# Pool starts moved by 128 bytes, and raw buffers taken from a ring, in a two-layer encoder kernel

## The chip, the cores and the metric

The kernel runs on one core of one Trainium2 chip. The metric is device time in microseconds: the median of several executions, and for the traces one execution that the hardware profiler recorded. A core has five engines with an instruction queue each: TensorE (PE; its weight loads are listed apart as PEld), VectorE (DVE), ScalarE (ACT), GpSimd (POOL) and SyncE (SP, which here issues nearly all DMAs).

## The reference

Two layers over 256 tokens of width 2048, in fp32. Each layer has a token mixer and a gated feed-forward, both between RMS norms, with a residual:

```python
x = x + rms_norm_post(mixer(rms_norm_pre(x)))
x = x + rms_norm_post(conv_glu(rms_norm_pre(x)))

def conv_glu(h, w_up, conv_w, conv_b, w_down):      # width 5632
    u = h @ w_up
    gate, val = u[..., :D_FF], u[..., D_FF:]
    gate = depthwise_conv3(gate, conv_w, conv_b)
    return (gelu(gate) * val) @ w_down
```

Layer 0's mixer is dilated and grouped-query attention with one input and one output projection. Layer 1's is latent attention: `c = h @ w_in` gives a latent query (512 columns), a latent key-value (512) and a rotary key (64), which are normed and projected up; then come attention and the output projection.

## The kernel before

**Products.** An fp32 matrix is parted into a high and a low half (`hi`, `lo`), and each product is made of three matmuls: high by high, low by high, high by low (`mm3`, lines 219 to 221; in `down`, lines 1312, 1313 and 1315). In the token-major products (`proj_tok`, the output projections and `down`) the activations are the stationary operand, 128 columns at a time, and the weights stream past, 512 columns each: a row `ps<-whi,gh` has `whi` streaming and `gh` stationary. The stationary tiles are `xhl` (normed input of a sub-layer), `oh`/`ol` (heads of a mixer), `cq`/`ckv` (the latents), `gh`/`gl` (the feed-forward's gated values, nine tiles each, and `g_last` for the last two blocks) and `seven` (sums of token blocks, below). In `proj_t` (lines 236 and 238) the weights are stationary.

**Down.** The down product uses Strassen's scheme of seven products for 11 of its 22 pairs of row blocks in the first half of the columns (h = 0) and 13 in the second (h = 1). `block_sums` makes the sums of weight blocks beforehand and writes them to DRAM (`b`); `token_sums` makes the sums of token blocks on VectorE into `seven` tiles. Their homes are the `x` tiles and `xm` tiles of the pool `act` and the tile `st` of the feed-forward's own pool. `down_order` sets the order of the plain and the seven-product items; `units` are the indices of the seven-product items.

**Weights.** All weights come in chunks of 128 x 1024 in one list. `weights()` hands out the next chunk; ahead of it, `_split` parts three chunks: ScalarE casts `raw` to `whi` (line 159), VectorE subtracts to get `wlo` (line 154). `_load` issues the DMA of later chunks on SP (line 137) into one of four `raw` buffers, or one of the extra tiles listed in `self.more` (then called `raw_more`): in `down` the tiles `yf`, `gw`, `misc` of the feed-forward's pool, in the second half of `down` also `x1` to `x3` once their sums are used up (line 1320), and at mixer 1's start four tiles of its own pool (`oh2`, `ol2`, `oh3`, `ol3`). Which one is taken is a running count modulo the number of buffers (line 130).

**Pools.** `const`, `act`, `wp` and `small` are opened first and stay; each mixer and each feed-forward opens a pool after them (`mix0`, `ffn0`, `mix1`, `ffn1`), which starts where `small` ends. Tiles in `small` take a multiple of 32 bytes per partition, for each of their buffers. `pre_norm` takes four small columns there, one of them `floor` with four buffers (line 366). The stationary tiles in the late pools start 128 bytes past a multiple of 256 (`gh0` at 117632), those in `act` at a multiple.

**Order.** The tile framework sorts the instructions of each engine; a tile of a late pool can be written only when what lay there before was used for the last time. At mixer 1's start the first eight matmul groups read weights that were parted ahead into tiles of the feed-forward's pool (`ahead`), and the transposes of the new `x` (line 482) run between them.

Of the kernel before, what the change touches and what calls it, by code (L numbers as in the profile page):

```python
# [3 lines left out]

# [1 line left out]

# [54 lines left out]
class Model:  # L61
# [6 lines left out]
    def __init__(self, ctx, tc, a, out):  # L68
        self.tc, self.nc, self.a, self.out = tc, tc.nc, a, out
        self.soon, self.bg, self.running = [], deque(), []  # L70
        self.held = deque()
        self.gate, self.lead, self.led = (), None, 8
        pool = lambda name, **k: ctx.enter_context(tc.tile_pool(name=name, **k))
        self.const = pool("const", bufs=1)
        self.act = pool("act", bufs=1)
        self.wp = pool("wp", bufs=1)
        self.small = pool("small", bufs=2)
        self.ps = pool("ps", bufs=4, space=bass.MemoryType.PSUM)
        self.dram = pool("dram", bufs=1, space=bass.MemoryType.DRAM)
        self.blocks = {}  # L80
        self.more, self.turns = [], count()


    def now(self, gen, after=()):
# [41 lines left out]
    def _load(self, i):  # L126
        if i >= len(self.chunks) or i in self.loaded or i < self.at or i in self.made:
            return
        src = self.chunks[i]() if callable(self.chunks[i]) else self.chunks[i]
        turn = next(self.turns) % (4 + len(self.more))  # L130
        if turn < len(self.more):
            pool, tag = self.more[turn]
            raw = pool.tile([P, 1024], F32, tag=tag, name="raw_more", bufs=1)
        else:
            raw = self.wp.tile([P, 1024], F32, tag="raw", name="raw", bufs=4)
        raw = raw[:, :src.shape[-1]]
        self.nc.sync.dma_start(out=raw, in_=src)
        self.loaded[i] = raw
# [25 lines left out]
            return low  # L164

    def less(self):
        self.more = []

    def behind(self, instructions):

# [5 lines left out]
    def weights(self, upto=None):  # L176

        i = self.at
        if upto is None:
            upto = i + (2 if self.lead else 3)  # L180
            self.follow()
        for j in range(i, upto):
            self._split(j)
        for j in range(upto, i + 6 + len(self.more)):
            self._load(j) if j < upto + 4 + len(self.more) else None
        self.at += 1
        return self.made.pop(i)

# [161 lines left out]
    def pre_norm(self, sp=None):  # L350

        nc = self.nc
        yield
        ss = self.small.tile([P, 2, 4], F32, tag="ss", name="ss", bufs=2)
        for c in range(4):
            while self.led <= 2 * c:
                yield
            for t in range(2):
                with self.behind(self.gate):
                    self.square_sums(ss[:, t, c:c + 1], self.x[c][:, t, :])  # L360
            yield
        tot, v, s = self.col("tot", 2), self.col("prev", 2), self.col("pres", 2)
        self.r = self.col("prer", 2)
        nc.vector.tensor_reduce(out=tot, in_=ss, op=ALU.add, axis=AX.X)
        nc.vector.tensor_scalar(out=v, in0=tot, scalar1=1.0 / D, scalar2=EPS, op0=ALU.mult, op1=ALU.add)
        self.floor = self.col("floor", 2, 4)
        nc.vector.tensor_scalar(out=self.floor, in0=v, scalar1=EPS, scalar2=None, op0=ALU.mult)
        nc.scalar.activation(s, v, AF.Sqrt)
        self.heron(s, v, self.r)
# [556 lines left out]
    def mixer1(self, pre):  # L926
        nc, tc, a = self.nc, self.tc, self.a
        with tc.tile_pool(name="mix1", bufs=1) as sp:
            x, xs = self.x_parts(), self.xhl
# [9 lines left out]
            def latent(ps, row, out):  # L939
                g = sp.tile([P, 512], F32, tag="grow", name="grow", bufs=1)  # L940
                nc.sync.dma_start(out=g, in_=a["lat"][row:row + 1, :].broadcast_to([P, 512]))
                ss = self.small.tile([P, 2, 1], F32, tag="ls", name="ls", bufs=2)
                for t in range(2):
                    self.square_sums(ss[:, t, :], ps[t])
                rr = self.rstd_over(ss, self.r, 1, 512)
                whole = []
                for t in range(2):
                    y = sp.tile([P, 512], F32, tag="y", name="y", bufs=2)
                    nc.vector.scalar_tensor_tensor(out=y, in0=ps[t], scalar=rr[:, t, :], in1=g,
                                                   op0=ALU.mult, op1=ALU.mult)  # L950
                    whole.append(y)
                yield
                for k in range(0, 4, 2):
                    pt = self.psum("at").rearrange("p (i t) -> p i t", i=2)
                    for j in range(2):
                        for t in range(2):
                            self.turn_whole(pt[:, j, t * P:(t + 1) * P], whole[t][:, (k + j) * P:(k + j + 1) * P])
                    self.parted(out[:, k:k + 2, 0, :], out[:, k:k + 2, 1, :], pt)
# [81 lines left out]
                        yield  # L1040

            norm = self.now(self.pre_norm())
            self.more = [(sp, f"{n}{i}") for i in range(2, 4) for n in ("oh", "ol")]
            evq = self.evac(latent(self.proj_tok(KD, x, opening=True), 0, cq), 2, (norm,))
            evkv = self.evac(latent(self.proj_tok(KD, x, before={6: self.less}), 1, ckv), 2, (evq,))
            evkr = self.evac(evac_kr(proj_kr()), 1, (evkv,))
# [2 lines left out]
            for p in range(8):  # L1049
# [3 lines left out]
                if p % 2 == 0:  # L1053
                    v, v_gen = [], []
# [140 lines left out]
    def token_sums(self, seven, homes, gh, gl, upto, room, room_tag, bufs=1, pause=10):  # L1195

        def add(out, a, b, op=ALU.add):
            self.nc.vector.tensor_tensor(out=out, in0=a, in1=b, op=op)

        while len(seven) < upto:  # L1200
            p = len(seven)
            pool, tag, q = homes.pop(0)
            k = slice(2 * (p % 2), 2 * (p % 2) + 2 * q)
            tmp = room.tile([P, 2, 512 * q], F32, tag=room_tag, name="sums", bufs=bufs)
            add(tmp[:, 0], gh[p // 2][:, k].rearrange("p k t -> p (k t)").bitcast(F32),
                gl[p // 2][:, k].rearrange("p k t -> p (k t)").bitcast(F32))
            a = tmp[:, 0].rearrange("p (q k t f) -> p q k t f", q=q, k=2, t=2)
            s = tmp[:, 1].rearrange("p (q n f) -> p q n f", q=q, n=4)
            a11, a12, a21, a22 = (a[:, :, k, t] for t in range(2) for k in range(2))
            add(s[:, :, 0], a21, a22)  # L1210
            add(s[:, :, 1], s[:, :, 0], a11, ALU.subtract)
            add(s[:, :, 2], a11, a21, ALU.subtract)
            add(s[:, :, 3], a12, s[:, :, 1], ALU.subtract)
            yield
            home = pool.tile([P, q, 4, 2, P], F32R, tag=tag, name=f"seven{p}")
            self.parted(home[:, :, :, 0, :], home[:, :, :, 1, :], s)
            seven.extend(home[:, i] for i in range(q))
            for _ in range(pause):
                yield

    def down(self, gh, gl, post, pre, kept, seven, sums):
# [5 lines left out]
        m, gains = [], []  # L1227
        many = PAIRS[0 if pre else 1]

        self.more = [(self.room, t) for t in ("yf", "gw", "misc")]  # L1230

        def x_back():
            for c in range(4):
                self.x[c] = self.act.tile([P, 2, 512], F32, name=f"x{c}")
                nc.sync.dma_start(out=self.x[c], in_=kept[c])
# [52 lines left out]
        for h in range(2):  # L1288
            items = down_order(h, many[h])
            units = [n for n, item in enumerate(items) if item[0] == "seven"]  # L1290
# [4 lines left out]
            n = len(items) - held  # L1295
# [20 lines left out]
                return ins if group else None  # L1316

            for i in range(n):
                if h and i == units[20]:
                    self.more += [(self.act, f"x{c}") for c in (1, 2, 3)]  # L1320
                    self.now(sums(many[1], self.wp, "raw", 4))
                if h and i == units[-1] - 6:
                    self.more = []
                if h and i == units[-1]:
                    x_back()
                if i == units[0]:
                    banks += [self.psum("at") for _ in range(4)]
                w = self.weights()
                while items[i][0] == "seven" and len(seven) <= items[i][1]:
                    self.tick()  # L1330
                for t in range(2):
                    products(i, t, w)
                self.tick()
                if i == units[-1]:
                    m.append(self.act.tile([P, 2, 2, 512], F32, tag="xm2" if h else "xm3", name=f"m{h}"))
                    if h:
                        gains.append(self.gain_row(post, 3))
                    ended = self.now(done(h, 0, added(h, banks[4:])))
# [152 lines left out]
```

## Time and profile before

| | us |
|---|---|
| median of 3 runs | 2051.09 (2050.76 to 2052.47) |
| profiled execution | 2049.91 |
| its span, first to last instruction | 2047.8 |

The page of the profile gives, for each engine, busy time, its share of the span and the count of instructions; then the chain of work that ended last; then the costliest groups of instructions by line, engine, operation and tiles (`out<-in`), with busy time, the mean of one, and the idle time ahead of them with what ended it. Timeline rows read: start, duration, engine, line, operation, tiles, count, and in brackets the idle time before with what was waited for. "DMA to landing" rows of a view by tile give the time from a DMA's issue to its last byte, least, median and most. Durations of matmuls are modelled and overlap; the distance of two starts is recorded.

### The profile page before, as it was taken

How to read it: one execution, taken by the hardware profiler on the slowest of the kernel's cores; microseconds unless marked ns; L12 is line 12 of the kernel's file. 1: busy time of each engine (PE TensorE's matmuls, PEld its weight loads, DVE VectorE, ACT ScalarE, POOL GpSimd, SP SyncE). 2: the span in 40 equal slices, each digit the busy share in tenths (PEclk: the TensorE clock that was granted, in tenths of full speed). 3: DMA queues.
4: the chain of work that ended last, by engine and by line, in shares of the span. 5: the costliest groups of instructions: out<-in, count | busy, mean ns of one | idle time of the engine just before them, and what ended most of it. 6: DMA issues, size and time to landing. Idle time of an engine off the chain costs nothing.

```text
span 2047.8 us, 29869 instructions
## 1 busy us (share of the span) xinstructions
PE 2035.3 (99%) x10858; PEld 1737.3 (85%) x10858; DVE 1577.6 (77%) x2368; ACT 1177.0 (57%) x1837; POOL 0.2 (0%) x4
## 2 busy tenths in 40 slices
PE   9999999999999999999999999999999999999998
PEld 7888888888888888888778998888888888888886
DVE  6877757887777787868787875688877777797876
ACT  7654546655555555656665664565555555555664
POOL 0000000000000000000000000000000000000000
PEclk9999999999999999999999999999999999999999
DMA  9545566888888887888964445688888988878895
GB/s 335 181 149 162 164 195 232 297 277 327 296 300 307 287 316 268 272 291 300 350 215 167 137 129 168 200 303 290 307 291 294 317 290 310 298 253 278 293 370 192
DMA packets 152499, 532.83 MB, mean 260 GB/s; under 512 B 16928, under 2 KB 17440, under 8 KB 152352
## 3 DMA queue, kind: packets, MB, share of 16 engines
q1 hardware_dynamic: 152064, 530.65, 75.9%
q8 instruction: 85, 1.39, 0.3%
q14 instruction: 62, 0.51, 0.1%
q10 hardware_dynamic: 288, 0.28, 0.0%
HBM read 474.23 MB, written 56.62 MB: 259 GB/s over the span
## 4 chain that ended last, share of the span: by engine, by line
PE 98%; ACT 1%; DVE 0%; DMA 0%; issue 0%; DVEq 0%; SPq 0%
PE ps L236 31%; PE ps L238 15%; PE ps L221 8%; PE ps L219 8%; PE ps L220 8%; PE ps L1312 7%; PE ps L1313 7%; PE ps L1315 7%; PE ps L652 1%; PE ps L305 1%; PE ps L555 1%; PE ps L482 0%; PE ps L562 0%; DMA raw<-in_w_in 0%; ACT whi L159 0%; PE ps L988 0%
## 5 line engine op out<-in xcount | busy, mean ns | idle before, releaser
L154 DVE TENSOR_TENSOR wlo<-raw,whi 128x1024 fp32r<-128x1024 f32 (+1 forms) x667 | 793.4, 1198 | 343.0 <-ACT whi L159 338.5
L159 ACT CAST whi<-raw 128x1024 fp32r<-128x1024 f32 (+1 forms) x667 | 684.8, 1031 | 590.9 <-PE ps L236 296.6
L236 PE MATMUL ps<-xhl,whi 128*128 128x512 f32 x2752 | 952.6, 394 | 0.0
L238 PE MATMUL ps<-xhl,wlo 128*128 128x256 f32 x2752 | 757.5, 277 | 0.0
L236 PEld LDWEIGHTS ps<-xhl,whi 128*128 128x128 f32 x2752 | 513.9, 188 | 117.1
L238 PEld LDWEIGHTS ps<-xhl,wlo 128*128 128x128 f32 x2752 | 516.5, 188 | 2.6
L154 DVE TENSOR_TENSOR wlo<-raw_more,whi 128x1024 fp32r<-128x1024 f32 (+1 forms) x129 | 144.9, 1144 | 49.4 <-ACT whi L159 48.2
L159 ACT CAST whi<-raw_more 128x1024 fp32r<-128x1024 f32 (+1 forms) x129 | 124.8, 985 | 77.4 <-PE ps L1313 48.0
L1312 PE MATMUL ps<-whi,gh 128*128 128x512 f32 x400 | 158.2, 396 | 1.1 <-ACT whi L159 1.1
L1313 PE MATMUL ps<-whi,gl 128*128 128x512 f32 x400 | 158.2, 395 | 0.0
L219 PE MATMUL ps<-whi,xhl 128*128 128x512 f32 x336 | 132.3, 395 | 0.5 <-ACT whi L159 0.5
L220 PE MATMUL ps<-wlo,xhl 128*128 128x512 f32 x336 | 131.3, 391 | 0.0
L221 PE MATMUL ps<-whi,xhl 128*128 128x512 f32 x336 | 131.0, 391 | 0.1
L1315 PE MATMUL ps<-wlo,gh 128*128 128x512 f32 x400 | 129.1, 394 | 0.0
L1168 DVE TENSOR_TENSOR blocks<-blocks 128x1024 f32<-128x1024 f32 x144 | 124.5, 865 | 0.9
L219 PE MATMUL ps<-whi,oh 128*128 128x512 f32 x256 | 101.6, 397 | 0.0
L221 PE MATMUL ps<-whi,ol 128*128 128x512 f32 x256 | 101.0, 395 | 0.0
L220 PE MATMUL ps<-wlo,oh 128*128 128x512 f32 x256 | 101.0, 394 | 0.0
L1312 PEld LDWEIGHTS ps<-whi,gh 128*128 128x128 f32 x400 | 75.3, 188 | 19.3 <-ACT whi L159 2.2
L1313 PEld LDWEIGHTS ps<-whi,gl 128*128 128x128 f32 x400 | 75.4, 189 | 17.7
L1315 PEld LDWEIGHTS ps<-wlo,gh 128*128 128x128 f32 x400 | 75.2, 188 | 17.9 <-DVE wlo L154 0.3
L309 ACT COPY gw<-ps 128x256 f32<-128x256 f32 x176 | 64.3, 369 | 39.6 <-PE ps L236 31.2
(232 smaller groups left out, 2368.1 us busy)
## 6 DMA issues: line engine op xcount, KB each, us to landing
raw<-in_w_up SPq DMA_DIRECT2D x352, 512.0 KB, 5.1
blocks<-in_w_down SPq DMA_DIRECT2D x96, 512.0 KB, 6.1
b<-blocks SPq DMA_DIRECT2D x96, 512.0 KB, 5.3
raw<-in_w_in SPq DMA_DIRECT2D x84, 512.0 KB, 4.4
raw<-in_w_down SPq DMA_DIRECT2D x71, 512.0 KB, 5.6
raw<-in_w_out SPq DMA_DIRECT2D x64, 512.0 KB, 4.0
raw_more<-in_w_down SPq DMA_DIRECT2D x57, 512.0 KB, 5.5
raw<-b SPq DMA_DIRECT2D x51, 512.0 KB, 5.9
```

Source lines behind the costliest of these rows:

```text
L154: return nc.vector.tensor_tensor(out=lo[:, s], in0=raw[:, s], in1=hi[:, s].bitcast(F32), op=ALU.subtract)
L159: self.nc.scalar.copy(hi[:, s], raw[:, s])
L219: mm(ps, lh, rh, start=start, stop=False)
L220: mm(ps, lh, rl, start=False, stop=False)
L221: return mm(ps, ll, rh, start=False, stop=stop)
L236: ins = mm(out[i], hi[:, s[kk]], x(k), start=k == 0, stop=False, skip_group_check=opening)
L238: ins = mm(out[i][:, :T], lo[:, s[kk]], x(k)[:, :T], start=False, stop=k == nk - 1, skip_group_check=opening)
L309: self.nc.scalar.copy(b, ps[:, T:])
L1168: nc.vector.tensor_tensor(out=x[:, a:a + n], in0=x[:, b:b + n] if n > 512 else x[:, a:a + n], in1=x[:, a:a + n] if n > 512 else x[:, b:b + ...
L1312: mm(bank, xh, w[0][:, c], start=start, stop=False, skip_group_check=loose)
L1313: mm(bank, xl, w[0][:, c], start=False, stop=False, skip_group_check=loose)
L1315: ins = mm(bank, xh, w[1][:, c], start=False, stop=stop, skip_group_check=loose)
```

## The change

Three edits. First, `floor` is no column of its own any more: `prev` has four columns, of which the last two are the floor; 4 buffers of 32 bytes go from `small`, and every pool opened after it starts 128 bytes lower (`gh0` at 117504, a multiple of 256). Second, the count modulo the number of buffers gives way to a deque: `ring[0]` is taken and the ring turned by one; extra tiles are put in front of it (`extendleft`, so in reversed order), and `less()` makes a ring of the four raw buffers again. Third, in the second half of `down` the late token sums start at unit 13 (unit 20 before), with their temporary in `x1` and not in a raw buffer; they are finished at unit 17, where `x1` to `x3` join the ring. The count of instructions on PE, ACT and DVE stays.

```diff
-        self.more, self.turns = [], count()
+        self.ring = deque([None] * 4)
@@ _load
-        turn = next(self.turns) % (4 + len(self.more))
-        if turn < len(self.more):
-            pool, tag = self.more[turn]
+        if self.ring[0]:
+            pool, tag = self.ring[0]
             raw = pool.tile([P, 1024], F32, tag=tag, name="raw_more", bufs=1)
         else:
             raw = self.wp.tile([P, 1024], F32, tag="raw", name="raw", bufs=4)
+        self.ring.rotate(-1)
@@ less
-        self.more = []
+        self.ring = deque([None] * 4)
@@ weights
-        for j in range(upto, i + 6 + len(self.more)):
-            self._load(j) if j < upto + 4 + len(self.more) else None
+        for j in range(upto, min(i + 2, upto) + len(self.ring)):
+            self._load(j)
@@ pre_norm
-        tot, v, s = self.col("tot", 2), self.col("prev", 2), self.col("pres", 2)
+        tot, both, s = self.col("tot", 2), self.col("prev", 4), self.col("pres", 2)
+        v, self.floor = both[:, :2], both[:, 2:]
@@
-        self.floor = self.col("floor", 2, 4)
         nc.vector.tensor_scalar(out=self.floor, in0=v, scalar1=EPS, scalar2=None, op0=ALU.mult)
@@ mixer1
-            self.more = [(sp, f"{n}{i}") for i in range(2, 4) for n in ("oh", "ol")]
+            self.ring.extendleft((sp, f"{n}{i}") for i in range(2, 4) for n in ("oh", "ol"))
@@ token_sums
-            for _ in range(pause):
+            for _ in range(pause if len(seven) < upto else 0):
                 yield
@@ down
-        self.more = [(self.room, t) for t in ("yf", "gw", "misc")]
+        self.ring.extendleft((self.room, t) for t in ("yf", "gw", "misc"))
@@
-                if h and i == units[20]:
-                    self.more += [(self.act, f"x{c}") for c in (1, 2, 3)]
-                    self.now(sums(many[1], self.wp, "raw", 4))
+                if h and i == units[13]:
+                    late = self.now(sums(many[1], self.act, "x1"))
+                if h and i == units[17]:
+                    self.finish(late)
+                    self.ring.extendleft((self.act, f"x{c}") for c in (1, 2, 3))
                 if h and i == units[-1] - 6:
-                    self.more = []
+                    self.less()
```

The order moves at a few places. The rows give line, operation, tiles with their numbers, shape and what is waited for; lines of the changed kernel are one lower. SP's queue at mixer 1's start, before. `raw_10016` to `raw_10022` are chunks 4 to 7 of layer 1's input, `raw_more_10024` to `raw_more_10030` chunks 8 to 11:

```order
L137 DMA raw_10016<-in_w_in1 128x1024 [waits DMAHW2_49,DVE_49]
L137 DMA raw_10018<-in_w_in1 128x1024 [waits DMAHW7_49,DMAHW3_49,DVE_49]
L137 DMA raw_10020<-in_w_in1 128x1024 [waits DMAHW4_49,DVE_49]
L435 DMA gb_11904<-in_post 128x512
L137 DMA raw_10022<-in_w_in1 128x1024 [waits DMAHW5_49,DVE_49]
L435 DMA gb_11906<-in_post 128x512 [waits DVE_49]
L137 DMA raw_10171<-in_w_in1 128x1024 [waits DMAHW6_49,DVE_49]
L934 DMA tabC_10009<-in_ropeC 128x256 [waits PE_49]
L137 DMA raw_more_10024<-in_w_in1 128x1024
L137 DMA raw_more_10026<-in_w_in1 128x1024 [waits DMAHW7_49]
```

And after, where `raw_more_10014` to `raw_more_10020` are chunks 4 to 7:

```order
L136 DMA raw_10022<-in_w_in1 128x1024 [waits DMAHW2_49,DVE_49]
L136 DMA raw_10024<-in_w_in1 128x1024 [waits DMAHW7_49,DMAHW3_49,DVE_49]
L136 DMA raw_10026<-in_w_in1 128x1024 [waits DMAHW4_49,DVE_49]
L434 DMA gb_11901<-in_post 128x512
L136 DMA raw_10028<-in_w_in1 128x1024 [waits DMAHW5_49,DVE_49]
L434 DMA gb_11903<-in_post 128x512 [waits DVE_49]
L933 DMA tabC_10007<-in_ropeC 128x256 [waits PE_49]
L136 DMA raw_more_10014<-in_w_in1 128x1024
L136 DMA raw_more_10016<-in_w_in1 128x1024 [waits DMAHW6_49]
```

Chunks 4 to 7 moved behind `tabC`, the first DMA into mixer 1's pool, whose wait is one for PE; chunks 8 to 11 moved ahead of it.

SP's queue in the second half of layer 0's down, where `x1` to `x3` have just become extra buffers, before (`b01` are sums of weight blocks; tile numbers rise in the order in which the chunks are used):

```order
L137 DMA raw_9327<-in_w_down0 128x512 [waits DMAHW4_49,DVE_49]
L137 DMA raw_more_9333<-b01_7_7008 128x1024 [waits DMAHW3_49]
L137 DMA raw_more_9351<-b01_7_7008 128x1024 [waits PE_49]
L137 DMA raw_more_9372<-in_w_down0 128x512 [waits DMAHW5_49,PE_49]
L137 DMA raw_more_9384<-in_w_down0 128x1024 [waits DMAHW6_49,PE_49]
L137 DMA raw_more_9329<-in_w_down0 128x1024 [waits DMAHW7_49,DMAHW0_49,DVE_49]
L137 DMA raw_9396<-b01_8_7195 128x1024
```

And after:

```order
L136 DMA raw_9289<-in_w_down0 128x512 [waits DMAHW6_49,DVE_49]
L136 DMA raw_more_9301<-in_w_down0 128x1024 [waits PE_49]
L136 DMA raw_more_9303<-b01_6_6810 128x1024 [waits DMAHW7_49]
L136 DMA raw_more_9305<-b01_6_6810 128x1024 [waits DMAHW0_49]
L136 DMA raw_more_9307<-in_w_down0 128x512 [waits DMAHW1_49,DVE_49]
```

Before, `raw_more_9329` stood behind four loads that are used after it; after, the loads stand in the order of their use, and the extra tiles come three units earlier.

VectorE's queue at the start of layer 0's down, before (`sums` are token sums; `raw_8042` is chunk 5 of the down):

```order
L701 TENSOR_TENSOR g_last_8008<-misc_3141,g_last_8008 128x256 [waits Activation_49] x2
L154 TENSOR_TENSOR wlo_8108<-raw_8042,whi_8107 128x1024 [waits DMAHW1_49,PE_49]
L154 TENSOR_TENSOR wlo_8130<-raw_8044,whi_8129 128x1024 [waits DMAHW2_49,PE_49,Activation_49]
L1198 TENSOR_TENSOR sums_8240<-gh3_3125,gl3_3134 128x1024
L1198 TENSOR_TENSOR sums_8240<-sums_8240 128x2x128 [waits DVE_49]
L154 TENSOR_TENSOR wlo_8142<-raw_more_8046,whi_8141 128x1024 [waits DMAHW5_49,PE_49,Activation_49]
```

And after, where chunk 5 lies in `raw_more_8040`, the tile `misc`:

```order
L700 TENSOR_TENSOR g_last_8006<-misc_3140,g_last_8006 128x256 [waits Activation_49] x2
L1197 TENSOR_TENSOR sums_8238<-gh3_3124,gl3_3133 128x1024
L1197 TENSOR_TENSOR sums_8238<-sums_8238 128x2x128 [waits DVE_49]
L1197 TENSOR_TENSOR sums_8238<-sums_8238 128x2x128
L1197 TENSOR_TENSOR sums_8238<-sums_8238 128x2x128 [waits DVE_49] x2
L700 TENSOR_TENSOR seven6_8256<-sums_8238,seven6_8256 128x8x128 [waits Activation_49]
L1197 TENSOR_TENSOR sums_8391<-gh4_3125,gl4_3134 128x1024 [waits DVE_49]
L153 TENSOR_TENSOR wlo_8106<-raw_more_8040,whi_8105 128x1024 [waits DMAHW6_49,PE_49,Activation_49]
```

Chunk 5's subtraction moved behind the sums; its buffer is now the one that `g_last` is made from.

More of the change, by code (lines that the diff above doesn't have):

```diff
@@ L2 @@
 from contextlib import ExitStack
-from itertools import count
 import numpy as np
```

## The prediction

> **What bounds the kernel now.** I read the page first: busy shares, clock, and the chain of waits.
>
> ```profile
> span 2047.8 us, 29869 instructions
> PE 2035.3 (99%) x10858; PEld 1737.3 (85%) x10858; DVE 1577.6 (77%) x2368; ACT 1177.0 (57%) x1837; POOL 0.2 (0%) x4
> PEclk9999999999999999999999999999999999999999
> PE 98%; ACT 1%; DVE 0%; DMA 0%; issue 0%; DVEq 0%; SPq 0%
> ```
>
> TensorE is busy for 99% of the span at a full clock and makes up 98% of the chain that ended last. So a term of my sum is worth something only if it shortens the distance from one matmul's start to the next, or opens or closes a gap on TensorE. The page's busy time of one matmul (some 390 ns) is modelled and overlaps the next, so I take the **pitch**: first and last start of an unbroken run in the timeline of PE, divided by the steps between them. The table of windows gives the counts.
>
> ```profile
> 181.60 0.39 PE L219 MATMUL ps<-whi,xhl 128*128 128x512 f32 x1
> 197.71 0.39 PE L221 MATMUL ps<-whi,xhl 128*128 128x512 f32 x1
> 256.81 0.39 PE L219 MATMUL ps<-whi,oh 128*128 128x512 f32 x1
> 326.30 0.39 PE L221 MATMUL ps<-whi,ol 128*128 128x512 f32 x1
> 181.60:197.70 16.10, 16.10 (x73) 13.33 (x72) 11.42 (x16) 5.73 (x7) 0.00 (x0) 1.00 0.55 176
> 256.80:326.30 69.50, 69.50 (x301) 56.35 (x300) 38.13 (x43) 32.87 (x44) 0.00 (x0) 1.00 0.67 207
> ```
>
> (Columns of the last two rows: window, its length, busy time and count of PE, PEld, DVE, ACT, POOL, then clock, DMA share, GB/s.) Same three lines of code, same shape, no gap in either: 72 matmuls with xhl stationary start over 16.11 us, that is 16.11 / 71 = 226.9 ns each; 300 with oh and ol over 69.49 us, 69.49 / 299 = 232.4 ns. The stationary operand is the second name. In the program xhl starts at a multiple of 256 bytes in its partition, oh and ol 128 bytes past one. In the down product the same pair exists side by side: two tiles of one shape, used by the same lines, the first (seven8) at a multiple of 256, the second (seven10, in tile st of the feed-forward's pool) 128 past one.
>
> ```profile
> 913.78 0.39 PE L1315 MATMUL ps<-wlo,seven 128*128 128x512 f32 x1
> 915.82 0.40 PE L1315 MATMUL ps<-wlo,seven 128*128 128x512 f32 x1
> 929.02 0.39 PE L1315 MATMUL ps<-wlo,seven 128*128 128x512 f32 x1
> 931.11 0.39 PE L1315 MATMUL ps<-wlo,seven 128*128 128x512 f32 x1
> ```
>
> Nine steps each: 2.04 / 9 = 226.7 ns and 2.09 / 9 = 232.2 ns. Hence **5.4 ns a matmul** hang on something that these two classes differ in. The confound: in the kernel before, every stationary operand that lies 128 past a multiple also lies above 117 KB in the partition, and every one at a multiple lies below 54 KB. The trace cannot part alignment from height; for alignment speaks that the slow pitch is flat over that height (232.4 with oh and ol, 232.2 with seven10).
>
> **Term 1, the shift.** Merging the column floor into prev takes 4 buffers of 32 bytes out of the small pool, so every pool opened after it (mixers and feed-forwards) starts 128 bytes lower: gh0 goes from 117632 to 117504 = 459 x 256, and with it gl, st, g_last, oh, ol, cq, ckv and the 256-column operands. What uses them 512 wide, from the groups by line:
>
> ```profile
> L1312 PE MATMUL ps<-whi,gh 128*128 128x512 f32 x400 | 158.2, 396 | 1.1 <-ACT whi L159 1.1
> L219 PE MATMUL ps<-whi,oh 128*128 128x512 f32 x256 | 101.6, 397 | 0.0
> L1312 PE MATMUL ps<-whi,g_last 128*128 128x512 f32 x64 | 25.4, 398 | 0.0
> L219 PE MATMUL ps<-whi,ckv 128*128 128x512 f32 x32 | 12.7, 398 | 0.0
> L219 PE MATMUL ps<-whi,cq 128*128 128x512 f32 x16 | 6.5, 405 | 0.0
> ```
>
> Each has two sister lines with the same count (each product of the program is made of three): 3 x (400 + 256 + 64 + 32 + 16) = 2304. The 72 with seven10 and some 64 steps that lead from an aligned operand into one of these bring 2440. At the difference of the long runs that is 2440 x 5.4 = 13.2 us. The shorter pair allows less within its rounding: (0.05 - 0.01) / 9 = 4.4 ns, 10.7 us. Short runs with waits between them are what the down consists of, so I take the middle, **-12.0 us** (-13.2 to -10.7). The 2752 matmuls of L236 keep their addresses. No other engine's durations hang on this: a subtraction takes 1.22 us from a raw tile of either class.
>
> A rule speaks against this term. The Trainium skill, "TensorE: Matmul & The Clock Gate", section "Step-by-step: what each phase is for", gives TensorE two independent SBUF read ports, one for the streamed operand, one for weight loads, so that loading the next tile takes nothing from the running matmul. By it the place of a stationary operand changes no pitch and term 1 is zero (rival A). The rows above disagree: 5.4 ns at equal loads and shapes.
>
> **Term 2, a late load that goes.** The old turn counter is taken modulo a length; when three tiles join in the second half of layer 0's down, the order jumps, and one load is issued five issues late (the order rows of the change show raw_more_9329).
>
> ```profile
> 983.03 0.33 SPq L137 DMA_DIRECT2D raw_more<-in_w_down  x1
> 987.67 2.00 ACT L159 CAST whi<-raw_more 128x1024 fp32r<-128x1024 f32 x2 [5.29 <-PE ps L1315]
> 987.25 0.39 PE L1315 MATMUL ps<-wlo,seven 128*128 128x512 f32 x1
> 988.77 0.50 PE L1312 MATMUL ps<-whi,gh 128*128 128x512 f32 x1 [1.14 <-ACT whi L159]
> ```
>
> ScalarE sat idle for 5.29 us, last for this load, and TensorE's step here is 1.52 us against 0.23: 1.29, with 0.1 behind it **-1.4 us**. The ring loads in turn, and no other cast in that half keeps TensorE waiting, so I see nothing late next. The sums that move from unit 20 to 13 are the same instructions, and the three tiles they join with were read for the last time two units earlier: nothing, or at worst the 0.3 us of a wait (kept in the range).
>
> **Term 3, a new wait at mixer 1's opening.** In the kernel before, weight chunks 4 to 7 of layer 1's input go into the four raw tiles and are there by 1062.82, where the cast starts. In the changed one the ring gives them the four tiles of mixer 1's own pool; these loads stand on SP behind tabC, the first DMA into that pool, which waits for TensorE's last use of the feed-forward's tiles.
>
> ```profile
> 1065.14 0.33 SPq L137 DMA_DIRECT2D raw<-in_w_in  x1
> 1065.59 0.36 SPq L934 DMA_DIRECT2D tabC<-in_ropeC  x1
> 1065.99 1.92 SPq L137 DMA_DIRECT2D raw_more<-in_w_in  x4
> DMA to landing us min/median/max: 3.7/3.7/3.7
> DMA to landing us min/median/max: 5.3/5.3/5.3
> 1062.82 1.99 ACT L159 CAST whi<-raw 128x1024 fp32r<-128x1024 f32 x2
> 1065.75 0.48 PE L219 MATMUL ps<-whi,xhl 128*128 128x512 f32 x1
> 1069.97 0.39 PE L219 MATMUL ps<-whi,xhl 128*128 128x512 f32 x1
> ```
>
> (The landing rows are those of the raw load at 1065.14 and of the first raw_more load at 1065.99.) Today chunk 4 starts on TensorE at 1065.75 and chunk 5 at 1069.97. After, chunk 4's load is issued at 1065.99 at the earliest, with nothing queued ahead, and lands 3.7 to 5.3 us later (as the raw load did; as the raw_more one did, which had that load ahead of it): 1069.7 to 1071.3. Cast 1.05, low part 1.22: its third matmul, the first with the low part, can start at 1072.0 to 1073.6, and the ten from there on at 0.23 bring chunk 5 to 1074.3 to 1075.9. That is 4.3 to 5.9 us late, all of it on TensorE. I take **+4.8**, nearer the unloaded row. Queued behind on ScalarE is nothing that TensorE needs sooner. Later the same stage gives something back:
>
> ```profile
> 1085.41 1.41 DVE L949 SCALAR_TENSOR_TENSOR y<-ps,rr,grow 128x512 f32<-128x512 f32 x2 [0.99 <-DMA grow<-in_lat]
> 1086.26 0.30 PE L305 MATMUL ps<-ident,y 128*128 128x128 f32 x1 [0.92 <-issue]
> ```
>
> This 0.9 us waits for grow, which will be there; but y's transposes now come 5 matmuls sooner after the products, so I book **-0.3** (-0.9 to +0.3).
>
> **Term 4, the two down starts.** Extra tiles now come first in the ring, the last-freed one (misc) first of all. In layer 0 chunk 5's load therefore waits for the last read of misc, and on DVE the sums move ahead of its subtraction.
>
> ```profile
> 822.11 0.39 PE L1312 MATMUL ps<-whi,gh 128*128 128x512 f32 x1
> 828.08 0.75 DVE L701 TENSOR_TENSOR g_last<-misc,g_last 128x256 fp32r<-128x256 f32 x2
> 834.66 0.39 PE L1312 MATMUL ps<-whi,gh 128*128 128x512 f32 x1
> 1822.58 1.05 ACT L159 CAST whi<-raw_more 128x1024 fp32r<-128x1024 f32 x1 [1.86 <-DMA raw_more<-in_w_down]
> 1823.68 0.50 PE L1312 MATMUL ps<-whi,gh 128*128 128x512 f32 x1
> DMA to landing us min/median/max: 5.6/5.6/5.6
> ```
>
> The read ends at 828.83; with 3.7 us to land (the free queue above) or 5.6 (the load of this chunk in layer 1, the last row) and a cast of 1.05, whi is there at 833.6 to 835.5. TensorE wants it 12.5 us after the down's start, at 834.66, and 0.25 us sooner by term 1; its low part, 1.22 us behind whi, it wants four matmuls later. So 0 to 1.5 us; I take **+1.0**, near the slow end, since layer 1 has this order already, and there the cast at 1822.58 waited for the load, and TensorE for the cast (the row at 1823.68 is stretched to 0.50). In layer 1 that stall grows by what TensorE gains ahead of it, 54 steps of 5 ns: **+0.25**.
>
> **The sum.** -12.0 - 1.4 + 4.8 - 0.3 + 1.0 + 0.25 = **-7.65 us** on the profiled execution (2049.91 us, its span 2047.8). That run lies 1.2 us under the median of 2051.09; the median then comes to **2043.4 us**. The best ends (-13.2 - 1.4 + 4.3 - 0.9 + 0 + 0.2) give -11.0, the worst (-10.7 - 1.1 + 5.9 + 0.3 + 1.5 + 0.4) -3.7: 2040.1 to 2047.4.
>
> **Rivals.** A: *the place does nothing.* The 5.4 ns belong to height, or to which operand the products take, and the pools end 128 bytes lower without result; this is also the case that the change does not do what it says. What is left is term 3, whose price then decides: -1.4 + 4.8 - 0.3 + 1.25 = +4.35, **2055.4, slower**. It turns from "no change" to "slower" where chunk 4's load lands after about 1069.9. For it speaks the confound and the rule cited; against it seven8 beside seven10.
> B: *the opening's loads are covered.* If tabC's release comes earlier than today's 1065.59, by as much as chunk 4 needs, term 3 vanishes: **2038.6**. Against it: the release is TensorE's own matmul, four transposes ahead of chunk 4.
> C: *VectorE takes over in the downs.*
>
> ```profile
> 822.10:837.70 15.60, 15.60 (x70) 12.65 (x69) 15.57 (x26) 9.72 (x16) 0.00 (x0) 1.00 0.78 255
> ```
>
> In a down's first 15.6 us DVE is busy 15.57. Were it so throughout, the gain on the downs' 1530 or so matmuls (7.5 us) would turn into waits: 2050.9; for half of them, **2047.2**. Over the whole span DVE has 77%, so only stretches can go this way.
>
> **How the numbers follow.** Forecast 0.68, A 0.17, B 0.07, C 0.08. 0.2% is 4.1 us, about what a measurement here can tell from no change: faster is under 2047.0, slower above 2055.2. The forecast's interval lies below 2047.0 but for its last tenths, so faster gets 0.66 + 0.07 + 0.02 = 0.75; A splits at its bound, slower 0.10; the rest, 0.15, is same. The range takes in the forecast, B and C, 0.83 in all: 2038.6 to 2051.
>
> **What would show it.** Right: unbroken runs with oh, ol, gh, gl at 227 ns and L236's pairs unchanged; no idle row at TensorE near 987; a gap of 4 to 6 us on TensorE ahead of chunk 4 of layer 1's input, ended by a cast whose load was issued behind tabC; a cast waiting for raw_more at layer 0's down start. Wrong: pitch still 232 (then A), no gap at the opening (B), or new waits of TensorE for wlo in the downs (C).

## The result

| | us | ratio to before, 95% interval |
|---|---|---|
| before, 5 runs | 2052.47 (2050.76 to 2055.09) | |
| changed, 5 runs | 2042.50 (2040.74 to 2043.64) | 0.9951 [0.9937, 0.9966] |
| forecast | 2043.4 (2038.6 to 2051.0) | |

The changed kernel is 0.5% faster. Its profiled execution took 2041.99 us, against 2049.91 before. Two further executions of the kernel before (2053.15 and 2055.09 us) are in its median here, which stood at 2051.09 when the forecast of -7.65 us was made; timed again beside one another (run 10), the two kernels are 7.7 us apart.

Page of the changed kernel:

```profile
span 2039.7 us, 29854 instructions
PE 2021.8 (99%) x10858; PEld 1737.4 (85%) x10858; DVE 1577.7 (77%) x2368; ACT 1177.8 (58%) x1837; POOL 0.2 (0%) x4
PE 95%; DVE 2%; DMA 2%; ACT 1%; issue 0%; SPq 0%; DVEq 0%; ACTq 0%
```

TensorE is still busy all along and DVE did nothing more; but 5% of the chain of waits now belongs to DMA, DVE and ACT, against 1% before. The span fell by 8.1 us, and the n-th matmul of one trace can be set against the n-th of the other, since both have 10858 (36 of them in another order). The lead is how much earlier the n-th matmul starts in the changed kernel; the texts below call this comparison "matched starts". Where the lead grows (-) and shrinks (+):

| stretch (time before, us) | lead, us |
|---|---|
| up to layer 0's down start (825) | -2.05 |
| its first chunks (825 to 840) | +0.54 |
| up to 983 | -3.07 |
| the place of the late load (983 to 990) | -1.50 |
| up to the end of that down | -1.19 |
| crossing into layer 1 (1045 to 1049) | +0.91 |
| mixer 1's opening (1061 to 1094) | +4.84, with -0.11 ahead of it |
| mixer 1, its projection and feed-forward | -1.90 |
| into layer 1's down (1781 to 1831) | -0.20 |
| the rest of it | -4.36 |

The gains lie where stationary tiles of the late pools are used, and at the place of the late load; the losses lie at three places. Runs with oh and ol, and the nine steps with seven10, in the timeline of PE of the changed kernel:

```profile
256.43 0.40 PE L218 MATMUL ps<-whi,oh 128*128 128x512 f32 x1
324.23 0.40 PE L220 MATMUL ps<-whi,ol 128*128 128x512 f32 x1
925.51 0.39 PE L1314 MATMUL ps<-wlo,seven 128*128 128x512 f32 x1
927.55 0.39 PE L1314 MATMUL ps<-wlo,seven 128*128 128x512 f32 x1
```

67.80 / 299 = 226.8 ns and 2.04 / 9 = 226.7 ns, where it was 232.4 and 232.2. The losses, as PE's and ACT's timelines show them (two rows of layer 0's down start, one of layer 1's, three of the crossing, the rest of the opening; SP's issue of tabC and DVE's x are among them):

```profile
831.91 2.95 ACT L158 CAST whi<-raw_more 128x1024 fp32r<-128x1024 f32 x3 [1.79 <-DMA raw_more<-in_w_down]
833.01 0.50 PE L1311 MATMUL ps<-whi,gh 128*128 128x512 f32 x1 [0.51 <-ACT whi L158]
1820.10 0.50 PE L1311 MATMUL ps<-whi,gh 128*128 128x512 f32 x1 [0.18 <-ACT whi L158]
1038.29 1.05 ACT L158 CAST ahead<-raw 128x1024 fp32r<-128x1024 f32 x1 [1.80 <-DMA raw<-in_w_in]
1041.53 1.42 DVE L473 SCALAR_TENSOR_TENSOR x<-m,postr,x 128x512 f32<-128x512 f32 x2
1042.34 0.66 PE L481 MATMUL ps<-ident,x 128*128 128x128 f32 x4 [0.85 <-DVE x L473]
1059.13 0.33 SPq L933 DMA_DIRECT2D tabC<-in_ropeC  x1
1063.39 1.04 ACT L158 CAST whi<-raw_more 128x1024 fp32r<-128x1024 f32 x1 [0.42 <-DMA raw_more<-in_w_in]
1064.49 0.73 PE L218 MATMUL ps<-whi,xhl 128*128 128x512 f32 x2 [4.51 <-ACT whi L158]
1065.75 0.79 PE L219 MATMUL ps<-wlo,xhl 128*128 128x512 f32 x1 [0.53 <-DVE wlo L153]
1066.77 0.63 PE L218 MATMUL ps<-whi,xhl 128*128 128x512 f32 x1
1067.19 0.63 PE L219 MATMUL ps<-wlo,xhl 128*128 128x512 f32 x1
1068.84 0.39 PE L218 MATMUL ps<-whi,xhl 128*128 128x512 f32 x1
1069.52 0.39 PE L218 MATMUL ps<-whi,xhl 128*128 128x512 f32 x1
```

tabC is issued at 1059.13, 6.46 us sooner than before (1065.59), so that much was TensorE's lead; chunk 5 starts at 1069.52 against 1069.97, a lead of 0.45. So 6.0 us are lost here. There are two parts: 4.51 and 0.53 us of waiting for chunk 4, whose load came behind tabC, and then a slow clock: from 1065.75 to 1068.84 seven steps take 3.09 us, where seven at 0.227 take 1.59, and the step from 1066.77 to 1067.19 is 0.42. The table of windows shows what share of the full clock was granted (third number from the end: 0.83, then 0.54, and 0.50 over the stretch of 3.41 us in which it was low):

```profile
1064.00:1066.00 2.00, 0.99 (x3) 0.55 (x4) 1.53 (x2) 2.00 (x5) 0.00 (x0) 0.83 0.93 377
1066.00:1069.00 3.00, 3.00 (x8) 2.38 (x9) 2.63 (x6) 2.99 (x7) 0.00 (x0) 0.54 0.95 288
1065.30:1068.71 3.41, 2.96 (x7) 2.38 (x8) 3.04 (x7) 3.40 (x8) 0.00 (x0) 0.50 0.94 321
```

The Trainium skill, "TensorE: Matmul & The Clock Gate", section "HAM oscillation — how this bites in real kernels", says that idle gaps of over some 3.4 us put TensorE back to half its clock. This gap of 4.5 us agrees. It isn't a bound from below, though: in run 5 half the clock followed a gap of 2.35 us.

### The profile page after: what moved, and what is told of

Read it like the earlier page. It is cut to its first block, busy times and chain, and to the rows that moved or that the text cites. A ratio compares the mean times of both kernels' runs of the same rounds, so it can differ in the third digit from the quotient of the medians.

```text
span 2039.7 us, 29854 instructions
## 1 busy us (share of the span) xinstructions
PE 2021.8 (99%) x10858; PEld 1737.4 (85%) x10858; DVE 1577.7 (77%) x2368; ACT 1177.8 (58%) x1837; POOL 0.2 (0%) x4
## 4 chain that ended last, share of the span: by engine, by line
PE 95%; DVE 2%; DMA 2%; ACT 1%; issue 0%; SPq 0%; DVEq 0%; ACTq 0%
PE ps L235 30%; PE ps L237 15%; PE ps L219 9%; PE ps L220 8%; PE ps L218 8%; PE ps L1311 7%; PE ps L1312 7%; PE ps L1314 7%; PE ps L651 2%; PE ps L304 1%; PE ps L554 1%; DVE wlo L153 1%; DMA raw_more<-in_w_down 1%; DMA raw<-in_w_in 0%; PE ps L481 0%; PE ps L561 0%
## 5 line engine op out<-in xcount | busy, mean ns | idle before, releaser
L153 DVE TENSOR_TENSOR wlo<-raw,whi 128x1024 fp32r<-128x1024 f32 (+1 forms) x659 | 783.5, 1197 | 341.3 <-ACT whi L158 334.9
L158 ACT CAST whi<-raw 128x1024 fp32r<-128x1024 f32 (+1 forms) x659 | 676.4, 1032 | 575.7 <-PE ps L235 301.0
L235 PE MATMUL ps<-xhl,whi 128*128 128x512 f32 x2752 | 952.6, 394 | 0.0
L237 PE MATMUL ps<-xhl,wlo 128*128 128x256 f32 x2752 | 757.5, 277 | 0.0
L235 PEld LDWEIGHTS ps<-xhl,whi 128*128 128x128 f32 x2752 | 513.9, 188 | 116.9
L237 PEld LDWEIGHTS ps<-xhl,wlo 128*128 128x128 f32 x2752 | 516.7, 188 | 2.6
L153 DVE TENSOR_TENSOR wlo<-raw_more,whi 128x1024 fp32r<-128x1024 f32 (+1 forms) x137 | 154.0, 1144 | 42.9 <-ACT whi L158 38.2
L158 ACT CAST whi<-raw_more 128x1024 fp32r<-128x1024 f32 (+1 forms) x137 | 134.0, 990 | 78.8 <-PE ps L1312 58.3
```

The source lines that it names most:

```text
L153: return nc.vector.tensor_tensor(out=lo[:, s], in0=raw[:, s], in1=hi[:, s].bitcast(F32), op=ALU.subtract)
L158: self.nc.scalar.copy(hi[:, s], raw[:, s])
L235: ins = mm(out[i], hi[:, s[kk]], x(k), start=k == 0, stop=False, skip_group_check=opening)
L237: ins = mm(out[i][:, :T], lo[:, s[kk]], x(k)[:, :T], start=False, stop=k == nk - 1, skip_group_check=opening)
```

## The experiments

Two questions were open. Does the shift bring the gain, and why (alignment of the stationary tile, its height, something else)? And what do the ring and the moved sums cost or save, each alone? Runs 1 to 4, 5 to 8 and 9 to 11 were timed in three sessions, each with the kernel before beside them (medians of 2050.83, 2050.78 and 2050.53 us). Each ratio is against that median; a difference to the changed kernel is one to its 2042.50 us, which run 10 found at 2042.83.

**1. The shift taken back.**

```diff
-        tot, both, s = self.col("tot", 2), self.col("prev", 4), self.col("pres", 2)
-        v, self.floor = both[:, :2], both[:, 2:]
+        tot, v, s = self.col("tot", 2), self.col("prev", 2), self.col("pres", 2)
+        self.floor = self.col("floor", 2, 4)
```

> The changed kernel with floor as a column of its own again: every late pool lies 128 bytes past a multiple of 256, as before; ring and sums stay as changed. Alignment theory: unbroken runs on oh, ol, gh and gl go back to 232 ns, and the time rises by 2440 x 5.3 = about 13 us over the changed kernel, to 2055 us, slower than the kernel before by 3 to 4 us (the price of the ring). Rival (the ring and the moved sums brought the gain, the place nothing): 2042.5 us and runs at 227 ns.

Measured 2055.51 us, 1.0021 [1.0012, 1.0031] of before: 13.0 us above the changed kernel's median (12.8 above run 4, which has the changed kernel's time and stood beside it), and slower than before. The run with oh and ol is back at 69.49 / 299 = 232.4 ns:

```profile
256.87 0.39 PE L218 MATMUL ps<-whi,oh 128*128 128x512 f32 x1
326.36 0.39 PE L220 MATMUL ps<-whi,ol 128*128 128x512 f32 x1
```

So the whole gain is the shift's; the rest of the change costs.

**2. The shift alone**, on the kernel before.

```diff
-        tot, v, s = self.col("tot", 2), self.col("prev", 2), self.col("pres", 2)
+        tot, both, s = self.col("tot", 2), self.col("prev", 4), self.col("pres", 2)
+        v, self.floor = both[:, :2], both[:, 2:]
...
-        self.floor = self.col("floor", 2, 4)
```

> The kernel before with only floor merged into prev: late pools at multiples of 256, buffers by turn and sums as before. Alignment theory: 12 to 13 us less than before, about 2039 us, 3 to 4 us less than the changed kernel; TensorE's stalls stay where the kernel before has them (987, 1085), and none of 4.5 us ahead of chunk 4. Rival (shift without effect): about 2052 us.

Measured 2038.00 us, 0.9943 [0.9928, 0.9957]: faster than the whole change. What TensorE waited for, by the view of waits (total, times, longest):

```profile
PE ps L1312 <- ACT whi L159: 3.4, 2, 2.8
```

The longest is the late load of the old turn counter, now 2.8 us where it was 1.1 before: TensorE comes to it sooner. There is no wait for a chunk at mixer 1's opening. Steps under 0.3 us alone, without the waits, add up to 13.6 us less than before by matched starts; that is the shift's own price.

**3. A shift of 64 bytes** on the changed kernel (and **4** and **9** in the same manner, each one line in `run`):

```diff
+        self.small.tile([P, 16], F32, name="pad", bufs=1)
```

> The changed kernel with 64 bytes of padding in the small pool: late pools 64 bytes past a multiple of 256. If only multiples of 256 are fast: runs on oh, ol, gh and gl at 232 ns and some 13 us more than the changed kernel, about 2055 us. If any multiple of 64 is fast and 128 is bad for another reason: 227 ns and 2042.5 us.

Measured 2057.26 us, 1.0032 [1.0020, 1.0044]; the run with oh and ol takes (326.14 - 256.37) / 299 = 233.4 ns:

```profile
256.37 0.40 PE L218 MATMUL ps<-whi,oh 128*128 128x512 f32 x1
326.14 0.39 PE L220 MATMUL ps<-whi,ol 128*128 128x512 f32 x1
```

So a multiple of 64 is not enough.

**4. Everything at 128.**

```diff
+        self.const.tile([P, 32], F32, name="pad")
```

> The changed kernel with 128 bytes of padding in the first pool: every stationary tile, the low ones too (xhl, the seven tiles, whi and wlo), lies 128 bytes past a multiple of 256. Alignment theory: runs on xhl and on all seven tiles also at 232 ns, and if L235's wide matmul pays too, 6700 x 5.3 = some 35 us over the changed kernel, about 2078 us; if only the runs of 512 columns pay, about 2063 us. Height theory (tiles above 117 KB are slow unless moved down by 128 bytes): xhl and the low seven tiles stay at 227 ns, L235's pairs at 347 ns, and the time is at most 2055 us.

Measured 2042.67 us, 0.9962 [0.9949, 0.9974], the changed kernel's time. Neither theory had foreseen it: with everything 128 bytes past a multiple of 256, none of these runs is slow.

```profile
181.65 0.40 PE L218 MATMUL ps<-whi,xhl 128*128 128x512 f32 x1
197.77 0.40 PE L220 MATMUL ps<-whi,xhl 128*128 128x512 f32 x1
256.48 0.40 PE L218 MATMUL ps<-whi,oh 128*128 128x512 f32 x1
324.28 0.40 PE L220 MATMUL ps<-whi,ol 128*128 128x512 f32 x1
```

16.12 / 71 = 227.0 ns and 67.80 / 299 = 226.8 ns. oh and ol lie at the same addresses as in run 1, where they took 232.4 ns. So neither the place of the stationary tile nor its height decides. New theory: what counts is the stationary tile's place **against that of the streamed one** (whi, wlo), both modulo 256.

**9. The weights at 128** with the late pools, xhl and the low seven tiles left at multiples, as a test of it:

```diff
+        self.wp.tile([P, 32], F32, name="pad")
```

> The changed kernel with 128 bytes of padding at the start of the weights' pool: whi, wlo and every late pool lie 128 bytes past a multiple of 256; xhl and the seven tiles with homes in act stay at multiples. If only the difference between the stationary tile's place and the streamed tile's counts: oh, ol, gh, gl, g_last, cq, ckv and seven10 (now both at 128) run at 227 ns, xhl and the low seven tiles (0 against 128) at 232: 1560 x 5.3 = 8.3 us over the changed kernel, 2050.8 us; if L235's wide matmul pays as well, 14.6 us more, 2065.4 us. If a place at 128 past a multiple is slow by itself: gh and oh at 232, xhl at 227, about 2055 us.

Measured 2064.12 us, 1.0065 [1.0051, 1.0079], with L235's share in it (2065.4 expected). Now xhl is slow, 16.50 / 71 = 232.4 ns, and oh is fast, 67.80 / 299 = 226.8 ns:

```profile
184.36 0.39 PE L218 MATMUL ps<-whi,xhl 128*128 128x512 f32 x1
200.86 0.39 PE L220 MATMUL ps<-whi,xhl 128*128 128x512 f32 x1
260.18 0.40 PE L218 MATMUL ps<-whi,oh 128*128 128x512 f32 x1
327.98 0.39 PE L220 MATMUL ps<-whi,ol 128*128 128x512 f32 x1
```

The two runs of all these kernels side by side (place modulo 256 of stationary / streamed tile, ns a step):

| kernel | xhl | | oh, ol | |
|---|---|---|---|---|
| before | 0 / 0 | 227.0 | 128 / 0 | 232.4 |
| changed | 0 / 0 | 227.1 | 0 / 0 | 226.8 |
| 3 | 0 / 0 | 227.1 | 64 / 0 | 233.4 |
| 4 | 128 / 128 | 227.0 | 128 / 128 | 226.8 |
| 9 | 0 / 128 | 232.4 | 128 / 128 | 226.8 |

Equal places are fast and unequal ones slow, in all ten. The run of 21 matmuls at mixer 1's start in which `ahead`, a tile of the late pool, streams against xhl bears it out: 233 ns a step before (128 streamed against 0) and in run 9 (128 against 0), 227 ns in the changed kernel and in run 4, where the two are equal. It also shows a limit. In run 3, where `ahead` lies at 64 and xhl at 0, the step is (1058.66 - 1054.07) / 20 = 229.5 ns, and not the 233.4 ns of oh at 64 against weights at 0:

```profile
1054.07 0.39 PE L218 MATMUL ps<-ahead,xhl 128*128 128x512 f32 x1
1058.66 0.39 PE L220 MATMUL ps<-ahead,xhl 128*128 128x512 f32 x1
```

So at a distance of 64 it matters which of the two is moved. Distances other than 0, 64 and 128 were not tried. In proj_t, where the weights are the stationary operand and xhl streams, the pairs of L235 and L237 took 12.0 us more in run 9 than in the changed kernel (matched starts over the stretches that hold the 2752 pairs, so 4.3 ns each).

**5. Mixer 1: raw buffers first.**

```diff
-            self.ring.extendleft((sp, f"{n}{i}") for i in range(2, 4) for n in ("oh", "ol"))
+            self.ring.extend((sp, f"{n}{i}") for i in range(2, 4) for n in ("oh", "ol"))
```

> The changed kernel with mixer 1's four extra tiles put behind the raw buffers in the ring, so that chunks 4 to 7 are loaded into raw buffers ahead of tabC, as before. My theory (the wait on the late pool costs what the trace of the changed kernel shows there): the gap of 4.5 us ahead of chunk 4 and the slow clock behind it go, grow's wait of up to 1 us comes back, some 4.8 us less than the changed kernel: 2037.7 us. Rival (loads of the opening are late anyway, since the crossing itself has them late): under 2 us less, with a new gap at chunks 8 to 11.

Measured 2039.87 us, 0.9946 [0.9931, 0.9961]: 2.6 us less than the changed kernel, not 4.8. In the trace the opening itself is 5.6 us shorter by matched starts, and the gap is gone; but at layer 0's down start, ahead of the edit and in the same instructions as in the changed kernel, this execution lost 3.35 us more (timeline of PE and ACT):

```profile
834.87 0.50 PE L1311 MATMUL ps<-whi,gh 128*128 128x512 f32 x1 [2.35 <-ACT whi L158]
833.77 2.95 ACT L158 CAST whi<-raw_more 128x1024 fp32r<-128x1024 f32 x3 [3.24 <-DMA raw_more<-in_w_down]
```

The table of windows has the clock at 0.71 behind that gap:

```profile
834.50:837.00 2.50, 2.13 (x6) 1.69 (x7) 2.15 (x2) 2.50 (x4) 0.00 (x0) 0.71 0.00 2
```

The load of chunk 5 landed late, 6.9 us after its issue, against 5.5 us in the changed kernel's trace. So what the down's ring costs is not the same in each execution.

**6. Down starts: raw buffers first.**

```diff
-        self.ring.extendleft((self.room, t) for t in ("yf", "gw", "misc"))
+        self.ring.extend((self.room, t) for t in ("yf", "gw", "misc"))
```

> The changed kernel with yf, gw and misc put behind the raw buffers in the ring at both down starts. My theory (chunk 5's load waits for the last read of misc): TensorE's idle time at the sixth chunk of both downs (0.5 us in layer 0, 0.2 in layer 1, 1.1 us with the stretched steps behind) goes, 2041.4 us. Rival (DVE's order, sums ahead of the subtraction, makes the stall): the idle time stays, 2042.5 us.

Measured 2039.83 us (2039.57 to 2040.50), 0.9948 [0.9933, 0.9963]: 2.7 us less than the changed kernel. TensorE has no idle row at either down start; by matched starts with the changed kernel 0.92 us in layer 0 and 0.61 in layer 1 are gone. The median gains more than that, as it would if the wait is often longer than in the one trace compared.

**7. Both**, the edits of 5 and 6.

> Both: raw buffers first in mixer 1 and at the down starts. If the two costs are separate they add: 4.8 + 1.1 us less than the changed kernel, 2036.6 us, and less than the shift alone by 1 to 2 us, since the load out of turn near 987 (2.8 us idle with the shift alone) is gone. Rival (one hides behind the other): 2037.7 us.

Measured 2034.86 us, 0.9924 [0.9909, 0.9939], and **11**, timed again beside the changed kernel:

> Raw buffers first in mixer 1 and at the down starts, timed once more beside the changed kernel: 2035 us again, 7 to 8 us less than the changed kernel.

2035.73 us, 0.9925 [0.9913, 0.9938], where the changed kernel (run 10) took 2042.83. The gain over the changed kernel is 7.1 to 7.6 us, more than the 2.6 and 2.7 us of runs 5 and 6 together, so neither cost hides behind the other. Run 5's trace still held a longer wait at the down start; whether that makes the difference was not shown. This version beats both kernels, and the shift alone by 2 to 3 us. TensorE's waits in run 7:

```profile
PE ps L304 <- issue: 1.5, 1, 1.5
PE ps L481 <- DVE x L473: 1.4, 2, 1.1
PE ps L218 <- ACT whi L158: 0.3, 1, 0.3
```

What is left is the wait for grow (L304), which came back, and the one for the new x (L481) at the crossing; the third row lies at the kernel's own start.

**8. Late sums at unit 20 again.**

```diff
-                if h and i == units[13]:
-                    late = self.now(sums(many[1], self.act, "x1"))
-                if h and i == units[17]:
-                    self.finish(late)
-                    self.ring.extendleft((self.act, f"x{c}") for c in (1, 2, 3))
+                if h and i == units[20]:
+                    self.ring.extendleft((self.act, f"x{c}") for c in (1, 2, 3))
+                    self.now(sums(many[1], self.wp, "raw", 4))
```

> The changed kernel with the late token sums back at unit 20 in a raw buffer and x1 to x3 joining the ring there. My theory (the move changes the order and timing of the last loads of layer 0's down, so that the cast of a weight chunk for layer 1 holds up the new x): the 0.85 us wait of TensorE for x at 1041 goes, 2041.5 us, and no stall returns near 987, since the ring keeps the turn. Rival (the wait comes from the faster TensorE alone): it stays, 2042.5 us.

Measured 2043.32 us, 0.9966 [0.9954, 0.9977]: no gain. At the crossing TensorE waited 0.2 us and not 0.85, and by matched starts 0.69 us came back; but 0.63 was lost near 991, where I expected nothing. The moved sums thus trade one wait for another. The crossing's wait also moved between 0.6 and 1.1 us in runs 5 to 7, 10 and 11 (0.3 in run 4), with the sums where the change puts them. It takes the move and the faster steps together: in run 1 (sums moved, slow steps) and in run 2 (fast steps, sums as before) TensorE has no such wait there. What sets its size stays open.

**10. The changed kernel again.**

> The changed kernel once more. Theory: the wait for chunk 5's load at the down starts (0.5 us idle in layer 0 in the first trace, 2.3 us in the same instructions ahead of the edit in the run with mixer 1's raw buffers first) falls differently in each execution; its median is 2042.5 us again, within 1.5 us, and the idle times at the two down starts differ from the first trace by some tenths or more, while those ahead of chunk 4 of layer 1's input stay at 4.3 to 4.8 us. Rival (the waits are fixed by the order): the same idle times within 0.1 us.

Measured 2042.83 us, 0.9964 [0.9951, 0.9978].

```profile
PE ps L218 <- ACT whi L158: 5.4, 2, 4.5
PE ps L1311 <- ACT whi L158: 1.1, 2, 0.6
```

Idle at the down starts 0.6 and 0.5 us (0.5 and 0.2 in the first trace), 4.5 ahead of chunk 4 again. The opening's wait came out at 4.4 to 4.8 us in all eight traces with this order; the down's goes with when a load lands. Behind the gap nine steps took 427 ns here, against five in the first trace.

## Why the prediction was right, and where its reasons were not

The forecast of 2043.4 us was 0.9 over the median. That it came so close is partly luck: a gain larger than booked and a loss that was not in the sum offset each other. Term by term:

- **Term 1 (-12.0, bounds -13.2 to -10.7).** The size is near: -13.0 by run 1, and -13.6 by run 2's steps without the waits, a little past the upper bound. That bound took 5.4 ns a step, where the long runs differ by 5.6; the lower end, from the short pair's rounding, was too careful. The reason failed. The step "stationary operands at a multiple of 256 are fast" holds only because whi and wlo are at one too (runs 4 and 9). The trace of before had the hint, in the first two rows below: the matmuls with `ahead` streaming, a tile in the late pool, took (1057.02 - 1052.36) / 20 = 233 ns a step with xhl at a multiple. I hadn't asked where the streamed operand lies. Rival A (the place does nothing) falls, and height with it. The two read ports of the Trainium skill, "TensorE: Matmul & The Clock Gate", section "Step-by-step: what each phase is for", don't keep the two operands' places from mattering together; why they do was not shown.
- **Term 2 (-1.4).** -1.5 over that place, of which 0.1 is pitch. Against the shift alone, the ring saves 3.1 us there by matched starts, since a faster TensorE waits longer for the late load. I had priced the stall at its size in the slower kernel.
- **Term 3 (+4.8, then -0.3).** 6.0 lost and 1.1 regained at grow: +4.84 net against +4.5. Mechanism and place are right (run 5). The terms inside are off: the load landed in 3.9 us, the quick end of my bounds, which alone would have made 4.5; the slow clock after the gap, 1.5 us, was not in the sum. grow's wait went whole. The two misses offset.
- **Term 4 (+1.0 and +0.25).** 0.92 in layer 0 and 0.61 in layer 1 (run 6); of the 0.61, the kernel before had 0.35 already. I gave one number to something that varies: the idle time in layer 0 was 0.5, 0.6, 1.6 and 2.35 us in four executions of the same instructions (the changed kernel twice, runs 8 and 5, whose edits come later), with 5.5, 5.2, 6.5 and 6.9 us from the load's issue to its landing, where I had taken 3.7 to 5.6.
- **Missing: the crossing (+0.9).** I had not asked what a TensorE some 7 us ahead at 1041 would wait for there. The trace of before shows casts of `ahead` waiting for loads at that place (third row below). The speed alone doesn't make the wait: in run 2 TensorE comes there 5.3 us ahead, with the sums as before, and doesn't wait. I had booked the moved sums at nothing, or 0.3 us at worst; together with the faster steps they cost this 0.9, of which run 8 got 0.7 back.
- **Rivals B and C.** B falls: tabC is released by the last matmul that reads `ahead`, and only transposes lie between it and chunk 4, eight in the changed kernel (four before). C falls too: DVE's load in the downs made no new wait of TensorE for wlo there.

```profile
1052.36 0.40 PE L219 MATMUL ps<-ahead,xhl 128*128 128x512 f32 x1
1057.02 0.39 PE L221 MATMUL ps<-ahead,xhl 128*128 128x512 f32 x1
1041.99 1.05 ACT L159 CAST ahead<-raw 128x1024 fp32r<-128x1024 f32 x1 [1.25 <-DMA raw<-in_w_in]
```

## What to carry to other kernels

Where matmuls run back to back, compare the start-to-start step of one shape between tiles, and look at the addresses of both operands; 128 bytes in a small pool were worth 13 us here. A gain of TensorE uncovers loads that were just in time, so price each late load against the faster engine, and put a buffer that comes free last at the end of a ring, not at its head. A change that bundles three edits should be taken apart: two lines of this one gave back 7 us.

## What the runs showed of the hardware that I had not expected

- In the unbroken runs, a 128x512 fp32 matmul with its weights loaded anew each time steps at 226.7 to 227.1 ns where the stationary and the streamed tile start at the same place modulo 256 bytes, and at 232.4 ns where they are 128 apart, whichever of the two is moved (233 with `ahead`). At 64 apart it steps at 233.4 ns with the stationary tile moved and at 229.5 ns with the streamed one (run 3).
- After 4.5 us without matmuls TensorE ran at half its clock for some time: 4 (run 6) to 10 (run 4) steps took 427 ns each, 1.5 us lost in the changed kernel. The granted clock was 0.50 for 3.41 us there and for twice that, 6.83 us, in run 10 (row below), with gaps of the same length. In run 5 a gap of 2.35 us was followed by seven such steps; in run 2 one of 2.8 us by none. So the length of the gap alone doesn't set the loss.

```profile
1063.30:1070.13 6.83, 5.83 (x13) 4.14 (x14) 5.53 (x10) 6.48 (x11) 0.00 (x0) 0.50 0.83 281
```
